# A hybrid decoder layer: convolutions in a lane of their own, longer pauses in the mixer's side work, retention by pairs of heads

## The chip, the cores and the metric

The kernel runs on one core of one Trainium2 chip. The metric is the device time of one execution in microseconds; the kernel before takes 2025.46 us in the median of three runs (2024.82 to 2027.49). Engines are named as in the profile: PE is TensorE (matmul), PEld its weight loads, DVE is VectorE, ACT is ScalarE, POOL is GpSimd, SP is SyncE, which issues most DMAs.

## The reference

One layer for 256 tokens with 2048 features, in float32:

```
x = x + 0.5 * swiglu(rmsnorm(x, n1), ffn1)          # width 5632
x = x + mixer(rmsnorm(x, n2), w_in, w_out)
x = x + 0.5 * swiglu(rmsnorm(x, n3), ffn2)
return rmsnorm(x, n4)

mixer: proj = h @ w_in; rq, rk, rv, rg (retention, 8 heads of 128), gq, gk, gv, gz (delta rule, 8 heads), ga, gb
  rq, rk = rotary(rq), rotary(rk) / sqrt(128)
  ro = layernorm_per_head(sum_{s<=t} gamma_h^(t-s) (q_t . k_s) v_s) * silu(rg)
  gq, gk, gv = silu(causal depthwise convolution over 4 tokens); q, k l2-normalised
  g = -exp(a_log) softplus(ga + dt_bias); beta = sigmoid(gb)
  S_t = exp(g_t) (I - beta_t k_t k_t^T) S_{t-1} + beta_t k_t v_t^T;  go_t = S_t^T q_t
  go = rmsnorm_per_head(go) * gw * silu(gz)
  return concat(ro, go) @ w_out
```

## The kernel before, in words

Every large product streams its weights. A piece of 512 KB (256 rows by 512 columns) is loaded by a DMA of SP into `raw`, ACT rounds it to `whi` (L134), DVE subtracts to get `wlo` (L135), and PE multiplies three times per 128 rows and token half: hi·hi, hi·lo, lo·hi (L148 to L150) into an `acc` bank. One such triple is called a unit here; a piece has four units, and pieces are prepared three ahead of PE. The first FFN comes first, then the mixer, then the second FFN.

The mixer has 16 column blocks of `w_in` of 32 units each, and then the output projection, 4 blocks of 32 units. Everything else in the mixer (convolutions, gates, delta rule, rotation, retention) is side work that rides along: it is written as generators, and after each unit `advance` lets each lane take a step. `yield n` in a generator means: nothing more for n units. Since all engines work in the order of the program, this fixes where each piece of side work stands between the matmuls. `until` advances the lanes without any unit between, when something is needed before the next block.

There are two lanes. `chains` holds, one behind the other, the gates, the three convolutions of head group 1 (K, Q, V; four heads), the delta chain of group 1, then the convolutions and the delta chain of group 2, and the chains that transpose the finished heads for the output projection. `side` holds the rotary tables, the rotation of retention's Q and K, and retention. So the three convolutions of group 2 begin when the delta chain of group 1 has ended, although their blocks may have been there for some time.

`evacuated` runs a block's 32 units and lets ACT write it to SBUF, in a ring of three `pe` buffers. A convolution (`conv_chain`) transposes two heads on PE into an `mx` bank (`mx` has three PSUM banks, `acc` four, `qd` one), ACT multiplies by the last tap (L705), DVE adds three taps per head (L707, runs of three), six units later the next two heads follow, each with its own Silu. The delta chain (`delta_chain`) first makes the decays: sixteen DVE instructions write `gu` (L750), two PE matmuls make `dp` from them (L754). Then come squares and norms, the matrices `Nt` and `At`, a recursion on DVE of two small instructions (`yn`, `Yb`, L837 and L838) per step and one step per unit, and two levels of a block inverse by quads: four `qd` matmuls (L808), one behind each unit (the trace has two records for each), and a DVE instruction that reads the bank: `Pm` (L862), then X or Y. At its end stand the states and the gate (L917). Retention takes its four heads at once.

In the output projection and the second FFN's start, steps of norms and transposes wait in the queue `later`, one of which is issued every second unit.

Of the kernel before, what the change touches and what calls it, by code (L numbers as in the profile page):

```python
# [85 lines left out]
def hybrid_layer(ctx: ExitStack, tc: tile.TileContext, a: dict, out: bass.AP):  # L86
# [10 lines left out]
    mx = ctx.enter_context(tc.tile_pool(name="mx", bufs=3, space=PSUM))  # L97
# [137 lines left out]
    def product(*args):  # L235
        accs, units = product_units(*args)
        for i, _ in enumerate(units):
            if i % 2 and i > 1 and later:
                later.popleft()()
        return accs  # L240
# [161 lines left out]
    def mixer_plan():  # L402
        wi, wo = a["w_in"][0], a["w_out"][0]
        half = RET_W // 2
        for c0 in ([O_GK, O_GQ, O_GV, O_GZ, O_GZ + half, O_RQ] + [o + half for o in (O_GK, O_GQ, O_GV)]
                   + [O_RK, O_RV, O_RG] + [o + half for o in (O_RQ, O_RK, O_RV, O_RG)]):
            whole(wi, rows_of(0, KD), c0)
        pair = [list(product_pieces(OUT_ORDER, wo, b * NB)) for b in range(2)]
        first = 3 * len(pair[0]) // 4
        for part in (slice(0, first), slice(first, None)):  # L410
            for b in range(2):
                stream.add((wo.tensor.name, b * NB), pair[b][part])
        for b in range(2, D // NB):
            whole(wo, OUT_ORDER, b * NB)
# [56 lines left out]
    with tc.manual_schedule(engines={E.PE, E.DVE, E.Activation}), tc.tile_pool(name="gd", bufs=1) as gd:  # L471
        gd.tile([P, PAD], F32, name="pad")

        def mixed_out(o, b, xt=None):
            for t in range(NT):
# [4 lines left out]
        env = dict(x_left=x_left, ident=ident, mx=mx, qd=qd, product=product, product_units=product_units, power=power,  # L480
                   split=split,
                   weight_piece=weight_piece, do_later=do_later, mixed_out=mixed_out,
# [33 lines left out]
def mixer(tc, a, gd, env):  # L516
    nc = tc.nc
    V, S, G, PE = nc.vector, nc.scalar, nc.gpsimd, nc.tensor
    x_left, ident, mx, qd, power = (env[k] for k in ("x_left", "ident", "mx", "qd", "power"))
# [7 lines left out]
    with ExitStack() as ctx:  # L527
# [19 lines left out]
        chains, side = deque(), deque()  # L547
        waits = {id(chains): 0, id(side): 0}

        def advance():  # L550
            for lane in (chains, side):
# [24 lines left out]
        rf, pes, read, PES = [], [], set(), 3  # L576

        def evacuated(col, dst=None, func=AF.Copy):
            ps, units = product_units(x_left, w_in, rows, col)
            run(units)  # L580
            if dst is None:

                until(lambda: len(pes) < PES or id(pes[-PES]) in read)
                dst = pb.tile([P, NT, NB], F32, name="pe", bufs=PES)
                pes.append(dst)
            for t in range(NT):
# [13 lines left out]
        def gates_chain():  # L600
# [21 lines left out]
            yield 7  # L622
# [6 lines left out]
            V.scalar_tensor_tensor(az, z, -1.0, z, ALU.mult, ALU.min)  # L629
            S.activation(az, az, AF.Exp)  # L630
# [4 lines left out]
            S.activation(az, az, AF.Ln, bias=ones)  # L635
            V.scalar_tensor_tensor(z, z, 0.0, az, ALU.max, ALU.add)
            for t in range(NT):
                V.scalar_tensor_tensor(g[:, t, :], z[:, t, :], -1.0, ea, ALU.mult, ALU.mult)
            S.copy(g2[:, 0], g)
            V.tensor_tensor(g2[:, 1], g, g2[:, 0].bitcast(F32), ALU.subtract)  # L640
            V.tensor_scalar(eb, eb, 1.0, None, ALU.add)
            V.reciprocal(beta, eb)

            yield 12
# [10 lines left out]
        def rotary_chain():  # L655
# [17 lines left out]
            for _ in range(2):  # L673
# [4 lines left out]
                for part in parts:  # L678
                    yield 4
                    for tx in (th.bitcast(F32), tl):  # L680
                        V.scalar_tensor_tensor(ang, tx, -part, ang, ALU.mult, ALU.add)
            V.tensor_scalar(ang, ang, -math.pi, math.pi, ALU.max, ALU.min)
            S.activation(sinT, ang, AF.Sin)
            V.scalar_tensor_tensor(ang, ang, -1.0, ang, ALU.mult, ALU.min)
            V.tensor_scalar(ang, ang, math.pi / 2, None, ALU.add)
            S.activation(cosT, ang, AF.Sin)
# [5 lines left out]
        def conv_chain(src, ct0, dst):  # L692
# [3 lines left out]
            dst = dst()  # L696
            for i in range(0, GH, 2):
                pt = mx.tile([P, 2, T], F32, name="mx")
# [3 lines left out]
                for j in range(2):  # L702
                    w = cw[:, ct0 + i + j, :]
                    yy = y[:, i + j, :]
                    S.mul(yy, pt[:, j, :], w[:, 3:4])  # L705
# [31 lines left out]
        gates, mixed = {}, []  # L737

        def delta_chain(gi, ins):

            hs = gi * GH
            kq, vT = ins["kq"], ins["vT"]
# [3 lines left out]
            for h0 in range(0, GH, 2):  # L746
# [4 lines left out]
                yield 2  # L751
# [6 lines left out]
            yield 4  # L758
# [3 lines left out]
            for c in range(NT):  # L762
                if c:
                    yield 2
# [4 lines left out]
            for c in range(NT):  # L769
                yield 2  # L770
                square_sums(tokens(qT, c), ss[:, 1, c * GH:(c + 1) * GH])
            V.tensor_scalar(ss, ss, EPS, None, ALU.add)
# [7 lines left out]
            for c in range(NT):  # L780
                yield 1
# [5 lines left out]
            for j in range(GH):  # L787
                yield 2
# [32 lines left out]
            Yb = gd.tile([P, B0 // RS, B0], F32, name="Yb")  # L821
# [11 lines left out]
            for j in range(B0 - 1):  # L833
# [5 lines left out]
                yield 1  # L839
            yd = dr.tile([NM, P, B0], F32, name="yd")  # L840
# [12 lines left out]
            for lev in range(LEV0, NLEV):  # L853
# [4 lines left out]
                yield 2  # L858
# [4 lines left out]
                if lev < NLEV - 1:  # L863
# [3 lines left out]
                    yield 2  # L867
# [18 lines left out]
            yield 2  # L886
            S.copy(st, four(lambda j: (kd[:, j, :], w[:, 0, j, :])))
            S.copy(o[:, 0], four(lambda j: (At[:, j, 0, :], w[:, 0, j, :])))
            yield 2
# [3 lines left out]
            V.tensor_tensor(o[:, 1], four(lambda j: (qT[:, j, P:], st[:, j, :])), eg1, ALU.mult)  # L893
            yield 3
            V.tensor_tensor(w[:, 1], four(lambda j: (Yv[:, j, 1, :], vh[:, 1, j, :])), bc(ck[:, 1, :]), ALU.mult)
            yield 2
# [22 lines left out]
        def delta_gate(gi):  # L919
            gates[gi] = zs = mk.tile([P, NT, NB], F32, name=f"gate{gi}")  # L920
            evacuated(O_GZ + gi * GW, zs, AF.Silu)
# [4 lines left out]
        def delta_products(gi):  # L926
            hs, cs = gi * GH, gi * GW
            ins = {}

            def kq(part):  # L930
                if part == 0:
                    ins["kq"] = gd.tile([P, GH, 2, T], F32, name="kq")
# [6 lines left out]
            chains.append(conv_chain(evacuated(O_GK + cs), 8 + hs, partial(kq, 0)))  # L939
            chains.append(conv_chain(evacuated(O_GQ + cs), hs, partial(kq, 1)))  # L940
# [180 lines left out]
```

## Time and profile before

| what | us |
|---|---|
| median of three runs | 2025.46 (2024.82 to 2027.49) |
| the profiled execution | 2025.33 |
| its span in the trace | 2023.6 |
| PE busy | 1972.1 |
| PE idle | 51.5 |
| DVE busy | 1289.1 |
| ACT busy | 888.5 |
| POOL busy | 59.7 |

The span is what the trace shows of one execution, the time has 1.7 us more outside it. Busy time is the union of an engine's instructions; the idle time in front of an instruction is put down to what released it. The granted clock of PE (PEclk) is a share of full speed: 1.00 is 2.4 GHz, 0.50 is 1.2 GHz.

### The profile page before, as it was taken

Reading aid. Unit: us, or ns where it says so; the run is one execution under the profiler, and the core shown is the slowest. Engines: PE = TensorE matmul, PEld = TensorE weight load, DVE = VectorE, ACT = ScalarE, POOL = GpSimd, SP = SyncE. Lnnn points to the kernel's source line nnn. Section 1 sums busy time; section 2 is a strip of 40 time slices with the busy share of each in tenths; the row PEclk is TensorE's granted clock in tenths of the full one; section 3 lists DMA queues with packets and bytes.
Section 4 is the critical chain, followed back from the end, with each engine's and each line's share of the span. In section 5 each row is a group of like instructions: output and inputs, shape, how many; then the busy total and the mean of one; then the engine's idle time right before and its main releaser. Section 6 shows DMA issues by size and latency. Waiting matters only on the chain.

```text
span 2023.6 us, 23594 instructions
## 1 busy us (share of the span) xinstructions
PE 1972.1 (97%) x8836; PEld 1620.1 (80%) x8836; DVE 1289.1 (64%) x1818; ACT 888.5 (44%) x1074; POOL 59.7 (3%) x79
## 2 busy tenths in 40 slices
PE   9999999999999999899799999999999999999998
PEld 7888888888888887777677778788888888888886
DVE  5776664456667766675668466866667554667654
ACT  6434433334443555543444344544444434444443
POOL 0000000000000000210021000000000000000000
PEclk9999999999999999999999999999999999999999
DMA  9666666666665655578447735666666666666564
GB/s 310 192 184 187 207 196 195 193 187 185 206 197 184 201 169 182 139 184 154 125 135 163 146 116 178 204 190 197 191 195 187 199 195 191 195 193 192 178 207 145
DMA packets 195267, 373.06 MB, mean 184 GB/s; under 512 B 14544, under 2 KB 15184, under 8 KB 195024
## 3 DMA queue, kind: packets, MB, share of 16 engines
q1 hardware_dynamic: 193888, 368.38, 62.0%
q0 software_dynamic: 832, 1.84, 0.4%
q8 instruction: 69, 1.13, 0.2%
q10 hardware_dynamic: 432, 1.34, 0.2%
q14 instruction: 46, 0.38, 0.1%
HBM read 368.89 MB, written 2.62 MB: 184 GB/s over the span
## 4 chain that ended last, share of the span: by engine, by line
PE 86%; DVE 8%; ACT 3%; issue 2%; DMA 1%; ACTq 0%; POOLq 0%; DVEq 0%
PE acc L148 28%; PE acc L149 27%; PE acc L150 27%; DVE wlo L135 3%; ACT whi L134 2%; DVE y L707 1%; PE qd L808 1%; DMA raw<-in_w_in_dram 1%; DVE y L253 1%; PE mx L731 1%; DVE yn L837 1%; DVE Yb L838 0%; PE mx L791 0%; DVE sq L253 0%; DVE ht L253 0%
## 5 line engine op out<-in xcount | busy, mean ns | idle before, releaser
L135 DVE TENSOR_TENSOR wlo<-raw,whi 128x1024 fp32r<-128x1024 f32 (+1 forms) x689 | 839.5, 1227 | 627.2 <-ACT whi L134 624.9
L134 ACT CAST whi<-raw 128x1024 fp32r<-128x1024 f32 (+1 forms) x689 | 718.4, 1050 | 814.1 <-PE acc L150 720.9
L148 PE MATMUL acc<-whi,xh 128*128 128x512 f32 x1920 | 763.5, 398 | 4.4 <-ACT whi L134 2.4
L149 PE MATMUL acc<-wlo,xh 128*128 128x512 f32 x1920 | 751.9, 392 | 5.0 <-DVE wlo L135 4.9
L150 PE MATMUL acc<-whi,xl 128*128 128x512 f32 x1920 | 750.7, 391 | 0.0
L149 PEld LDWEIGHTS acc<-wlo,xh 128*128 128x128 f32 x1920 | 362.8, 189 | 79.7 <-DVE wlo L135 8.9
L148 PEld LDWEIGHTS acc<-whi,xh 128*128 128x128 f32 x1920 | 362.8, 189 | 78.4 <-ACT whi L134 6.6
L150 PEld LDWEIGHTS acc<-whi,xl 128*128 128x128 f32 x1920 | 362.4, 189 | 76.2
L149 PE MATMUL acc<-wlo,hh 128*128 128x512 f32 x704 | 273.9, 389 | 0.0
L150 PE MATMUL acc<-whi,hl 128*128 128x512 f32 x704 | 273.9, 389 | 0.0
L148 PE MATMUL acc<-whi,hh 128*128 128x512 f32 x704 | 273.9, 389 | 0.0
L253 DVE STREAM_TRANSPOSE ht<-h 32x256 f32<-32x256 f32 x352 | 153.3, 436 | 5.3
L149 PEld LDWEIGHTS acc<-wlo,hh 128*128 128x128 f32 x704 | 132.1, 188 | 27.7 <-DVE wlo L135 0.2
L148 PEld LDWEIGHTS acc<-whi,hh 128*128 128x128 f32 x704 | 132.1, 188 | 27.5
L150 PEld LDWEIGHTS acc<-whi,hl 128*128 128x128 f32 x704 | 132.1, 188 | 27.3
L140 ACT CAST hh<-ht 128x512 fp32r<-128x512 f32 x44 | 27.2, 618 | 121.2 <-DVE ht L253 121.2
L149 PE MATMUL acc<-wlo,mh 128*128 128x512 f32 x96 | 37.7, 393 | 3.1 <-DVE wlo L135 3.0
L141 DVE TENSOR_TENSOR hl<-ht,hh 128x512 fp32r<-128x512 f32 x44 | 30.3, 688 | 15.1 <-ACT hh L140 15.1
L707 DVE SCALAR_TENSOR_TENSOR y<-mx,cw,y 128x255 f32<-128x255 f32 (+2 forms) x72 | 34.6, 481 | 8.2 <-ACT y L705 6.5
L347 ACT ACTIVATE sg<-acc,rfac 128x512 f32<-128x512 f32 x44 | 29.8, 689 | 18.4 <-PE acc L150 16.0
L148 PE MATMUL acc<-whi,mh 128*128 128x512 f32 x96 | 37.4, 390 | 0.0
L150 PE MATMUL acc<-whi,ml 128*128 128x512 f32 x96 | 37.4, 390 | 0.0
(210 smaller groups left out, 759.7 us busy)
## 6 DMA issues: line engine op xcount, KB each, us to landing
raw<-in_ffn_w_up_dram SPq DMA_DIRECT2D x176, 512.0 KB, 4.5
raw<-in_ffn_w_down_dram SPq DMA_DIRECT2D x176, 512.0 KB, 4.5
raw<-in_ffn_w_gate_dram SPq DMA_DIRECT2D x175, 512.0 KB, 4.4
raw<-in_w_in_dram SPq DMA_DIRECT2D x128, 512.0 KB, 4.8
raw<-in_w_out_dram SPq DMA_DIRECT2D x32, 512.0 KB, 3.7
x<-in_x_dram SPq DMA_DIRECT2D x4, 512.0 KB, 6.4
out_dram<-x SPq DMA_DIRECT2D x8, 256.0 KB, 2.4
h<-in_xt_dram SPq DMA_DIRECT2D x7, 256.0 KB, 5.8
```

The source lines that it names most:

```text
L134: S.copy(hi, raw)
L135: V.tensor_tensor(lo, raw, hi.bitcast(F32), ALU.subtract)
L140: S.copy(hi, src)
L141: V.tensor_tensor(lo, src, hi.bitcast(F32), ALU.subtract)
L148: PE.matmul(o, lhsT=sh, rhs=hi, start=first, stop=False)
L149: PE.matmul(o, lhsT=sh, rhs=lo, start=False, stop=False)
L150: PE.matmul(o, lhsT=sl, rhs=hi, start=False, stop=last)
L253: V.transpose(dv[q:q + Q, :, :, r:r + Q], sv[r:r + Q, :, :, q:q + Q])
L347: S.activation(sg[:, t, :], g[t], AF.Silu, scale=rf[:, t:t + 1])
L707: V.scalar_tensor_tensor(yy[:, lag:], pt[:, j, :T - lag], w[:, 3 - lag:4 - lag], yy[:, lag:], ALU.mult, ALU.add)
L731: PE.matmul(pt[:, j, :], lhsT=lhsT, rhs=rhs, start=True, stop=True)
L808: PE.matmul(pt[:m, i, :], lhsT=lhsT, rhs=rhs, start=True, stop=True)
```

## The change

A third lane, `convs`, holds the convolutions alone; they get a PSUM bank of their own, `cv` (one buffer), and `mx` has two banks instead of three. In a convolution ACT's multiplications of both heads come first, the two runs of three stand two and five units behind, the next pair eight units behind the first, and one Silu ends it. The delta chain is queued from the start and waits until its V is there; the second one stands behind the mixed chain of group 1. Most pauses get longer, by one unit or more, and the gates' chain and the rotary tables get pauses where there were none. The block order changes: the second half of GZ moves from ahead of RQ to behind the second group's convolution blocks and RK. The ring of evacuated blocks has two buffers, the two gates share one tile, and `delta_gate`, RV and RG are written to tiles that are asked for only after their units. Retention goes by pairs of heads and writes its result over `v`. The first two blocks of the output projection are walked in four parts by head group, each needing only the heads that it reads, and `later` gives a step every third unit.

```diff
-    mx = ctx.enter_context(tc.tile_pool(name="mx", bufs=3, space=PSUM))
+    mx = ctx.enter_context(tc.tile_pool(name="mx", bufs=2, space=PSUM))
+    cv = ctx.enter_context(tc.tile_pool(name="cv", bufs=1, space=PSUM))
...
+    def beside(units, every=2):
+        for i, _ in enumerate(units):
+            if (i + 1) % every == 0 and i > 1 and later:
+                later.popleft()()
...
-        for c0 in ([O_GK, O_GQ, O_GV, O_GZ, O_GZ + half, O_RQ] + [o + half for o in (O_GK, O_GQ, O_GV)]
-                   + [O_RK, O_RV, O_RG] + [o + half for o in (O_RQ, O_RK, O_RV, O_RG)]):
+        for c0 in ([O_GK, O_GQ, O_GV, O_GZ, O_RQ] + [o + half for o in (O_GK, O_GQ, O_GV)]
+                   + [O_RK, O_GZ + half, O_RV, O_RG] + [o + half for o in (O_RQ, O_RK, O_RV, O_RG)]):
...
-        chains, side = deque(), deque()
+        chains, convs, side = deque(), deque(), deque()
...
-        rf, pes, read, PES = [], [], set(), 3
+        rf, pes, read, PES = [], [], set(), 2
...
             for i in range(0, GH, 2):
-                pt = mx.tile([P, 2, T], F32, name="mx")
+                pt = cv.tile([P, 2, T], F32, name="cv")
                 for j in range(2):
                     for t in range(NT):
                         PE.transpose(pt[:, j, t * P:(t + 1) * P], src[:, t, (i + j) * P:(i + j + 1) * P], ident)
                 for j in range(2):
+                    S.mul(y[:, i + j, :], pt[:, j, :], cw[:, ct0 + i + j, 3:4])
+                if i + 2 == GH:
+                    read.add(id(src))
+                yield 2
+                for j in range(2):
                     w = cw[:, ct0 + i + j, :]
                     yy = y[:, i + j, :]
-                    S.mul(yy, pt[:, j, :], w[:, 3:4])
                     for lag in (1, 2, 3):
                         V.scalar_tensor_tensor(yy[:, lag:], pt[:, j, :T - lag], w[:, 3 - lag:4 - lag], yy[:, lag:],
                                                ALU.mult, ALU.add)
-                if i + 2 == GH:
-                    read.add(id(src))
-                    S.activation(dst, y, AF.Silu)
-                    held.discard("y")
-                yield 6
+                    yield 3
+            S.activation(dst(), y, AF.Silu)
+            held.discard("y")
...
             hs = gi * GH
+            while "vT" not in ins:
+                yield 1
...
-                yield 2
+                yield 4
                 dp = mx.tile([P, 4, P], F32, name="mx")
...
-            chains.append(conv_chain(evacuated(O_GK + cs), 8 + hs, partial(kq, 0)))
-            chains.append(conv_chain(evacuated(O_GQ + cs), hs, partial(kq, 1)))
-            chains.append(conv_chain(evacuated(O_GV + cs), 16 + hs, vT))
-            chains.append(delta_chain(gi, ins))
+            convs.append(conv_chain(evacuated(O_GK + cs), 8 + hs, partial(kq, 0)))
+            convs.append(conv_chain(evacuated(O_GQ + cs), hs, partial(kq, 1)))
+            convs.append(conv_chain(evacuated(O_GV + cs), 16 + hs, vT))
...
-        chains.append(gates_chain())
         side.append(rotary_chain())
-        delta_products(0)
+        chains.append(gates_chain())
+        chains.append(delta_chain(0, ins[0]))
+        delta_products(0, ins[0])
         delta_gate(0)
-        delta_gate(1)
+        chains.append(mixed_chain(NH, gates[0], ["kq"]))
         q0 = rotated(O_RQ, "rqT")
-        delta_products(1)
-        r0 = retention_products(0, q0)
-        chains.append(mixed_chain(NH, gates[0], ["kq"]))
+        delta_products(1, ins[1])
+        chains.append(delta_chain(1, ins[1]))
+        r0 = retention_products(0, q0, lambda: delta_gate(1))
...
-        for _, units in pair:
-            run(islice(units, 3 * GH * NT))
-        until(lambda: not chains and not side)
-        for b, (o, units) in enumerate(pair):
-            deque(units, 0)
-            env["mixed_out"](o, b, pb.tile([P, NB // P, T], F32, name="y" if b else "sq", bufs=1))
+        for i in range(4):
+            until(lambda: len(made) > i)
+            for b, (o, units) in enumerate(pair):
+                part = islice(units, GH * NT)
+                if i < 3:
+                    run(part)
+                    continue
+                env["beside"](part, 3)
+                env["mixed_out"](o, b, pb.tile([P, NB // P, T], F32, name="y" if b else "sq", bufs=1))
```

DVE's order ahead of group 2's `gu`, in the kernel before (L707 is a convolution's tap, L975 the rotation of a `pe` block, L135 the weight stream's subtraction):

```order
L707 SCALAR_TENSOR_TENSOR y<-mx,cw,y 128x255
L707 SCALAR_TENSOR_TENSOR y<-mx,cw,y 128x254
L707 SCALAR_TENSOR_TENSOR y<-mx,cw,y 128x253
L707 SCALAR_TENSOR_TENSOR y<-mx,cw,y 128x255
L707 SCALAR_TENSOR_TENSOR y<-mx,cw,y 128x254
L707 SCALAR_TENSOR_TENSOR y<-mx,cw,y 128x253
L135 TENSOR_TENSOR wlo<-raw,whi 128x1024
L975 TENSOR_TENSOR y<-pe,cosT 128x512 x2
L750 TENSOR_SCALAR gu<-cst,g_5470 128x128 x8
L135 TENSOR_TENSOR wlo<-raw,whi 128x1024
```

The two runs of three of the last pair stand directly ahead of a rotation and `gu`. DVE's order at the same `gu` (now L769) in the changed kernel (L142 splits the transposed heads of group 1 that the mixed chain makes, L787 makes `kd` from the keys):

```order
L938 SCALAR_TENSOR_TENSOR gate<-o,fac,gate 128x128 x8
L136 TENSOR_TENSOR wlo<-raw,whi 128x1024
L142 TENSOR_TENSOR m_7657<-mx,m_7657 128x512
L136 TENSOR_TENSOR wlo<-raw,whi 128x1024
L142 TENSOR_TENSOR m_7657<-mx,m_7657 128x512
L769 TENSOR_SCALAR gu<-cst,g_5473 128x128 x8
L136 TENSOR_TENSOR wlo<-raw,whi 128x1024
L769 TENSOR_SCALAR gu<-cst,g_5473 128x128 x8
L136 TENSOR_TENSOR wlo<-raw,whi 128x1024 x2
L787 TENSOR_TENSOR kd<-mx,eg 128x512
```

No convolution stands near `gu` any more; all of group 2's are far ahead of it. The first of them stands inside group 1's recursion; DVE's order there in the changed kernel, from the last tap of its first run of three to the last of its second (L857 and L858 are the recursion's step, L726 the tap, and behind the second run of three the bank `cv` is free for the next two heads):

```order
L726 SCALAR_TENSOR_TENSOR y<-cv,cw,y 128x253
L857 TENSOR_TENSOR yn<-Ub,Yb 128x75
L858 TENSOR_TENSOR Yb<-Yb,yn 128x5x15
L136 TENSOR_TENSOR wlo<-raw,whi 128x1024
L857 TENSOR_TENSOR yn<-Ub,Yb 128x70
L858 TENSOR_TENSOR Yb<-Yb,yn 128x5x14
L857 TENSOR_TENSOR yn<-Ub,Yb 128x65
L858 TENSOR_TENSOR Yb<-Yb,yn 128x5x13
L726 SCALAR_TENSOR_TENSOR y<-cv,cw,y 128x255
L726 SCALAR_TENSOR_TENSOR y<-cv,cw,y 128x254
L726 SCALAR_TENSOR_TENSOR y<-cv,cw,y 128x253
```

In the kernel before, the recursion has nothing between its steps but the weight stream (four steps, then L135); now the two runs stand between them.

PE's order where group 1's first quad ends and its second begins, in the kernel before (a `whi` with a new number is a new piece, `qd` with a new number is the next quad, which needs the bank that `Pm` has read):

```order
L808 MATMUL qd_7039<-X_7029,Nt_6378 128x64
L148 MATMUL acc_7016<-whi_6974,xh_93 128x512
L149 MATMUL acc_7016<-wlo_6975,xh_93 128x512
L150 MATMUL acc_7016<-whi_6974,xl_94 128x512
L808 MATMUL qd_7039<-X_7029,Nt_6378 128x64
L148 MATMUL acc_7015<-whi_6992,xh_93 128x512
L149 MATMUL acc_7015<-wlo_6993,xh_93 128x512
L150 MATMUL acc_7015<-whi_6992,xl_94 128x512
L808 MATMUL qd_7064<-X_7029,Nt_6378 128x64
```

The two quads meet at the end of a piece. PE's order at the same place in the changed kernel:

```order
L828 MATMUL qd_7196<-X_7177,Nt_6450 128x64
L149 MATMUL acc_7041<-whi_7144,xh_96 128x512
L150 MATMUL acc_7041<-wlo_7145,xh_96 128x512
L151 MATMUL acc_7041<-whi_7144,xl_97 128x512
L828 MATMUL qd_7196<-X_7177,Nt_6450 128x64
L149 MATMUL acc_7042<-whi_7144,xh_96 128x512
L150 MATMUL acc_7042<-wlo_7145,xh_96 128x512
L151 MATMUL acc_7042<-whi_7144,xl_97 128x512
L828 MATMUL qd_7221<-X_7177,Nt_6450 128x64
```

The first quad's last matmul, behind the fourth unit of a piece before, now stands behind the first, and the next quad's first one behind the second.

## Rows read from the trace of the kernel before

**Rows 1.** Page, busy time: us, share of the span, instructions.

```profile
PE 1972.1 (97%) x8836; PEld 1620.1 (80%) x8836; DVE 1289.1 (64%) x1818; ACT 888.5 (44%) x1074; POOL 59.7 (3%) x79
```

**Rows 2.** TensorE by stretch of the mixer: length, busy, granted clock, DMA share, GB/s.

```profile
760.00:780.00 20.00, 17.55 (x72) 0.91 0.47 142
...
980.00:1000.00 20.00, 17.66 (x84) 1.00 0.41 131
1000.00:1020.00 20.00, 7.19 (x21) 0.70 0.36 107
...
1180.00:1220.00 40.00, 36.73 (x188) 1.00 0.41 132
...
1260.00:1298.00 38.00, 33.88 (x146) 1.00 0.55 169
sum 571.00, PE 532.32; mean PE 31.31
```

**Rows 3.** The same table for five short stretches behind idle times.

```profile
774.90:778.30 3.40, 2.64 (x7) 0.63 0.37 81
823.50:829.80 6.30, 6.30 (x22) 0.73 0.74 139
1016.40:1021.40 5.00, 4.63 (x10) 0.50 0.44 149
1109.10:1112.50 3.40, 2.76 (x10) 0.67 0.98 236
1130.50:1133.90 3.40, 3.04 (x9) 0.53 0.88 169
```

**Rows 4.** Waits of TensorE in the mixer: us in total, times, longest.

```profile
PE mx L754 <- DVE gu L750: 16.5, 2, 11.5
PE acc L149 <- DVE wlo L135: 7.3, 7, 1.5
PE mx L987 <- DVE y L980: 4.0, 4, 2.1
PE qd L808 <- DVE Pm L862: 3.1, 2, 2.4
```

**Rows 5.** Timeline around 1016, VectorE, then TensorE: start, us, line, operation.

```profile
1007.61 1.51 DVE L707 SCALAR_TENSOR_TENSOR y<-mx,cw,y 128x255 f32<-128x255 f32 x3 [0.54 <-ACT y L705]
...
1015.76 1.65 DVE L750 TENSOR_SCALAR gu<-cst,g 128x128 fp32r<-128x128 f32 x8
...
1016.77 1.49 PE L754 MATMUL mx<-gu,slr 128*128 128x512 f32 x2 [11.47 <-DVE gu L750]
```

**Rows 6.** Timeline of TensorE at 815: two matmuls of the weight stream.

```profile
815.20 0.39 PE L149 MATMUL acc<-wlo,xh 128*128 128x512 f32 x1
815.42 0.39 PE L150 MATMUL acc<-whi,xl 128*128 128x512 f32 x1
```

**Rows 7.** Timeline of VectorE at 878: one step of the recursion.

```profile
878.06 0.23 DVE L837 TENSOR_TENSOR yn<-Ub,Yb 128x76 f32<-128x76 f32 x1
878.33 0.24 DVE L838 TENSOR_TENSOR Yb<-Yb,yn 128x76 f32<-128x76 f32 x1
```

**Rows 8.** Timeline at 1146: `whi`, `wlo`, `Pm`, the next `qd` matmul.

```profile
1145.19 1.05 ACT L134 CAST whi<-raw 128x1024 fp32r<-128x1024 f32 x1
...
1146.27 1.23 DVE L135 TENSOR_TENSOR wlo<-raw,whi 128x1024 fp32r<-128x1024 f32 x1 [2.47 <-ACT whi L134]
...
1147.41 0.42 DVE L862 TENSOR_TENSOR Pm<-qd,cst 128x256 f32<-128x256 f32 x1
...
1147.89 0.43 PE L808 MATMUL qd<-X,Nt 128*128 128x64 f32 x2 [0.69 <-DVE Pm L862]
```

**Rows 9.** Timeline of VectorE, 1187 to 1195: statistics, gate, scaling.

```profile
1187.07 0.26 DVE L1026 BATCH_NORM_STATS2 bs<-rd 128x6 f32<-128x128 f32 x1
...
1191.17 2.19 DVE L917 SCALAR_TENSOR_TENSOR gate<-o,fac,gate 128x128 f32<-128x128 f32 x8
1193.28 2.14 DVE L1036 TENSOR_SCALAR rd<-rd,mv,rs 128x128 f32<-128x128 f32 x8
```

More of the change, by code (lines that the diff above doesn't have):

```diff
@@ L233, in do_later, with product @@
             later.popleft()()
-    def product(*args):
+    def beside(units, every=2):
+        for i, _ in enumerate(units):
+            if (i + 1) % every == 0 and i > 1 and later:
+                later.popleft()()
+    def product(*args, every=2):
         accs, units = product_units(*args)
-        for i, _ in enumerate(units):
-            if i % 2 and i > 1 and later:
-                later.popleft()()
+        beside(units, every)
         return accs
@@ L404, in mixer_plan @@
         half = RET_W // 2
-        for c0 in ([O_GK, O_GQ, O_GV, O_GZ, O_GZ + half, O_RQ] + [o + half for o in (O_GK, O_GQ, O_GV)]
-                   + [O_RK, O_RV, O_RG] + [o + half for o in (O_RQ, O_RK, O_RV, O_RG)]):
+        for c0 in ([O_GK, O_GQ, O_GV, O_GZ, O_RQ] + [o + half for o in (O_GK, O_GQ, O_GV)]
+                   + [O_RK, O_GZ + half, O_RV, O_RG] + [o + half for o in (O_RQ, O_RK, O_RV, O_RG)]):
             whole(wi, rows_of(0, KD), c0)
         pair = [list(product_pieces(OUT_ORDER, wo, b * NB)) for b in range(2)]
-        first = 3 * len(pair[0]) // 4
-        for part in (slice(0, first), slice(first, None)):
+        n = len(pair[0]) // 4
+        for i in range(0, len(pair[0]), n):
             for b in range(2):
-                stream.add((wo.tensor.name, b * NB), pair[b][part])
+                stream.add((wo.tensor.name, b * NB), pair[b][i:i + n])
         for b in range(2, D // NB):
@@ L574, in hold, with evacuated @@
             held.add(name)
-        rf, pes, read, PES = [], [], set(), 3
-        def evacuated(col, dst=None, func=AF.Copy):
+        rf, pes, read, PES = [], [], set(), 2
+        def evacuated(col, dst=None, func=AF.Copy, free=None):
             ps, units = product_units(x_left, w_in, rows, col)
@@ L585, in evacuated @@
                 pes.append(dst)
+            else:
+                until(free)
+                dst = dst()
             for t in range(NT):
@@ L735, in b4 @@
             return ap.unsqueeze(1).broadcast_to([P, 4, ap.shape[1]])
-        gates, mixed = {}, []
+        gates, mixed, made = {}, [], []
         def delta_chain(gi, ins):
             hs = gi * GH
+            while "vT" not in ins:
+                yield 1
             kq, vT = ins["kq"], ins["vT"]
@@ L919, in delta_gate @@
         def delta_gate(gi):
-            gates[gi] = zs = mk.tile([P, NT, NB], F32, name=f"gate{gi}")
-            evacuated(O_GZ + gi * GW, zs, AF.Silu)
+            gates[gi] = zs = evacuated(O_GZ + gi * GW, partial(mk.tile, [P, NT, NB], F32, name="gate"), AF.Silu,
+                                       lambda: gi == 0 or id(gates[0]) in read)
             for c in range(NT):
@@ L962, in mixed_chain @@
             read.add(id(src))
+            made.append(r0)
         def rotated_chain(src, dst):
@@ L1044, in retention_chain @@
             gate.append(None)
+            done.append(hs)
         def rotated(col, name):
```

123 lines of the change are left out of this document (66 added, 57 removed).

## Prediction

> **What bounds the kernel now.** The page comes first: TensorE (PE) is busy 1972.1 of 2023.6 us [rows 1], so what the change can give is PE's idle time and the time in which PE ran slowly; the number of matmuls is the same in both kernels. The second view is the table of busy time by stretch. The mixer runs from 727 to 1298 us, and in these 571.0 us PE is busy 532.32, so 38.7 us of idle time lie there [rows 2], three quarters of all 51.5. The third view is the granted clock. In five stretches behind long idles PE is granted 0.50 to 0.73 of full speed; one minus the clock, times the length, gives 1.26 + 1.70 + 2.50 + 1.12 + 1.60 = 8.2 us [rows 3]. The mixer so loses about 47 us. More than that the change cannot give, since it touches nothing outside.
>
> The fourth view, PE's waits, says who ends the idle time [rows 4]: VectorE (DVE) every time that matters. DVE is not full (64%), it is handed much at once. The two waits for `gu` are the largest: 16.5 us, of which 11.5 in group 2 and so 5.0 in group 1 [rows 4]. In group 2 the DVE rows show why: the convolution's runs of three (1.51 us) stand in one row ahead of `gu`, with the `wlo` of the weight stream between, and PE's matmul L754 stands still until 1016.77 [rows 5]. Around it, 980 to 1020, PE is idle 2.3 + 12.8 = 15.1 us [rows 2].
>
> **The measure for what follows.** Matmuls of the weight stream start 0.22 to 0.23 us apart at full clock (815.20, 815.42), so a unit of three takes 0.68 us, a weight piece (4 units) 2.72 us [rows 6]. At 0.50 of the clock [rows 3] a matmul costs some 0.2 us more. A piece asks DVE for one `wlo` of 1.23 us, behind which the next instruction starts after 1.14 us [rows 8]; I count 1.13.
>
> **What is removed**, against the 47 us:
> - The row of convolutions, `gu` and L754 in group 2. A lane of their own starts the three convolutions as soon as their blocks are there, and `gu`, which only needs the gates, is issued four units (2.7 us) ahead of L754. 15.1 us idle and 2.5 us of clock go: 17.6.
> - `gu` in group 1: 5.0 idle and 1.7 clock, 6.7.
> - The gates' chain, now in small parts (stretch behind 772): 2.4 idle [rows 2], 1.3 clock, 3.7.
> - The first rotation behind the recursion, 1.6, and the second, 2.4 and 1.1 of clock: 5.1. The waits for `y` in [rows 4] are these.
> - The waits for `Pm` of group 2: 3.1 idle and 1.6 clock, 4.7 [rows 4, 3].
> - `wlo` late behind group 2's recursion: 0.9, one of the seven waits for it that sum to 7.3 [rows 4].
> - The end of the mixed transposes (`m`, `ml`, `pe`): 3.3 [rows 2], which moves and is counted again below.
> - The output projection: 38.0 less 33.88 busy leaves 4.1 [rows 2]; with the deferred steps every third unit (2.04 us) instead of every second (1.36) DVE gets what it needs.
> That is 46. The rest (0.4 at 743, where PE waits for ScalarE) stays.
>
> **What it adds.** None of the new waits stands in the trace of before; each is bounded by rows.
> - *One buffer for the convolutions' transposes (`cv`).* The second pair's transposes are issued 8 units (5.4 us) behind the first's, and the first pair's last run of three is issued at +5 units: 3 units (2.04 us) for 1.51 us of DVE [rows 5]. Alone that holds. A `wlo` of 1.13 between makes it 0.6 late, as soon as one falls there; for three of the six convolutions I take 0.45, and for group 1's second one, where a table load of ScalarE lies ahead, 1.1: 2.5. Bounds: nothing, and 1.13 each, 6.8.
> - *Group 2's first convolution lies over group 1's recursion.* A recursion step is `yn` and `Yb`, 0.27 each, one step a unit [rows 7]. Four steps and a `wlo` are 2.12 + 1.13 = 3.25 us for a piece of 2.72: DVE falls 0.53 us back in each piece, 2.7 us in the five pieces ahead of the convolution. From its first run of three to the end of its second DVE is handed five steps (2.65), one or two `wlo` (1.7) and two runs (2.9): 7.2 us, where PE's next `cv` transposes come 5.4 us behind. PE waits 2.7 + 7.2 − 5.4 = 4.5; I take 4.1, since not every instruction of these stretches follows without a pause on the one before. Behind a wait of 5.0 the clock cost 1.7 [rows 3]; I take 2. Sum 6.1; bounds 0 and 6.5.
> - *The quads of the triangular inverse (`qd`, one PSUM buffer).* In group 1 a quad's last matmul now stands behind the first unit of a piece and no longer behind the last, as the order of PE shows. At that place DVE has just begun the piece's `wlo` (ScalarE's `whi` starts with the piece and takes 1.05 [rows 8]), so `Pm` starts 2.25 us into the piece and ends at 2.67, while PE wants the buffer 1.84 us in. The nearest row is 1146 to 1148: there `wlo` came late, `Pm` stood behind it, and PE's next `qd` matmul waited 0.69, about 0.95 against its due place [rows 8]. Here it is 0.85 to 1.45 with a run of three between; six quads at 1.15 give 7. Bounds: 0 (if `Pm` comes first) and 9.
> - *The gate of group 2 and the transposes behind it.* In the 16 units (10.9 us) ahead, DVE is handed the statistics (eight of 0.26 with a short fold behind each, 3.2), the scaling L1056 (2.14 as L1036 in before), the gate's run of eight (2.19) [rows 9], the last product (two, 1.3) and four `wlo` (4.5) and some small ones: 14.5. Of the 3.6 excess I take 2.5 as idle, with 1.0 of clock: 3.5; 0.75 more for `mx` having two buffers. Bounds 0 and 6. Without any of it the removed 3.3 above is all gain.
> - The rest, all with DVE a little late: `dp` 0.7, `wlo` beside it 0.4, the rotations 0.7, the 0.4 that stays: 2.2.
> The sum is 2.5 + 6.1 + 7 + 4.25 + 2.2 = 22. The mixer's loss falls from 47 to 22, so 25 us are won: 2025.3 − 25 = **2000** us. The profiled execution is 0.1 us from the median of the runs shown, so no correction is made.
>
> *Costed at nothing:* the new order of the blocks with two buffers for evacuated blocks (a block's last reader is through before the second next one is evacuated, 64 units later), retention by pairs of heads (the same products, `o` written over `v`), the output projection's first pair in quarters (each quarter's operand is issued before the units that read it), and the weight stream on SP, whose pieces keep their number and lead: between 36 and 55% of the DMA time is used in the stretches shown [rows 2]. If a cover is gone, steps are issued with no units between them, as at 1005, at the price of that wait.
>
> **The rivals.**
> - *The new waits don't show.* DVE has 36% free, and PE takes the weights three pieces ahead. If the convolution, the quads and the gate cost nothing, 5 of the 22 are left: 1983. For it: in before the recursion put DVE some 4 us back (7.5 pieces by 0.53), which cost PE only 0.9. Against: here PE waits for the buffer itself.
> - *The clock.* Six idles of over 1 us in some 30 units, with the `cv` wait not far ahead, could take PE to 1.2 GHz for that stretch: 30 × 3 matmuls × 0.2 = 18 us more, 2018. Against it: PE's waits for `wlo` were up to 1.5 us long, two of these in the output projection, and the granted clock from 1260 to 1298 stayed 1.00 [rows 4, 2]; the half clock came behind idles of 2.1, 2.4, 5.0 and 11.5 us and behind 772's two that add up to 2.4. The Trainium skill ("TensorE: Matmul & The Clock Gate", section "A second HAM failure mode: psum-queue depth-cycling") tells of a kernel in which short idles between groups of matmuls, from cycling through PSUM buffers, made the clock go up and down and lowered the throughput; that speaks against fewer `mx` buffers and a single `cv`. By that rule the time is this rival's; the rows so far don't bear it out.
> - *The second `dp` still waits for `gu`*, so that the change does only half of what it says: as in group 1 of before, 5.0 + 1.7 = 6.7 more, 2007.
> - *Slower: the single `cv` buffer.* If each of the six convolutions pays the 6.1 that I give only to one, the sum grows by 5 × 6.1 − 2.5 = 28: 2028. It decides from 25/5 + 0.5 = 5.5 us for each of the other five. Against it: only one lies over a recursion.
>
> **How the numbers follow.** A measurement of this kernel tells about 0.2%, 4 us, from no change. Forecast (1994 to 2006) 0.47; new waits hidden (1981 to 1994) 0.20; `dp` again 0.08; the clock (2010 to 2019) 0.15; no change 0.05; slower 0.05. Forecast, hidden waits, `dp` and clock all end below 2021: faster 0.90. The range for 8 in 10 leaves out the best of the hidden case and the worst of the clock's with what lies above: 1984 to 2015; it holds the lower and most of the upper bounds above (0 and +6.5, 9, 6 against 6.1, 7, 4.25).
>
> **What would show it.** In the trace after: no wait for `gu` above 1 us, PE idle in the mixer near 18 and half clock for about 4; a wait of 3 to 5 us for `cv` at the first convolution of group 2, and some six waits near 1 us at L828 in group 1. The prediction is wrong where waits for `cv` come at every convolution, where the granted clock falls in group 1's quads, or where PE waits for `wlo` for microseconds, since then DVE is fuller than these rows say.

## The result and the profile after

The changed kernel takes 2003.74 us in the median of four runs (2002.66 to 2004.88), the kernel before 2026.47 in its four (2024.82 to 2027.74): a ratio of 0.9888, 95% interval 0.9871 to 0.9905, so 22.7 us faster. The forecast was 2000 with 1984 to 2015. The profiled execution took 2002.66 us, its span is 2000.8. One of the ten executions of the kernel with the lane undone, below, took 2828 us at a granted clock of 0.65, and its ratio leaves that one out.

The page's first lines of the changed kernel, as in [rows 1]:

```profile
span 2000.8 us, 23620 instructions
...
PE 1966.6 (98%) x8836; PEld 1618.0 (81%) x8836; DVE 1289.9 (64%) x1818; ACT 892.4 (45%) x1075; POOL 61.8 (3%) x79
```

PE's idle time is 2000.8 − 1966.6 = 34.2 us, where it was 51.5. The stretch that answers to 727 to 1298 now ends at 1276. The table by stretch of the changed kernel (length, busy, granted clock, DMA share, GB/s), to be read beside [rows 2, 3]:

```profile
885.00:900.00 15.00, 11.69 (x48) 0.89 0.75 136
...
930.00:968.00 38.00, 32.76 (x166) 1.00 0.52 124
...
1000.00:1020.00 20.00, 18.09 (x80) 0.91 0.48 139
...
1085.00:1100.00 15.00, 11.69 (x50) 0.99 0.75 170
1100.00:1115.00 15.00, 15.00 (x63) 0.90 1.01 181
...
1180.00:1200.00 20.00, 18.23 (x88) 1.00 0.45 155
...
1240.00:1276.20 36.20, 36.20 (x162) 1.00 0.64 208
sum 549.20, PE 527.18; mean PE 27.75
```

In 549.2 us PE is busy 527.18: 22.0 us idle, where it was 38.7. The clock costs 0.11 × 15 + 0.09 × 20 + 0.01 × 15 + 0.10 × 15 = 5.1, where it was 8.2. The loss fell from 47 to 27 us. These 20 us explain most of the 22.7. About 1 us lies outside the mixer (1452.6 us there before, 1451.6 now), and the other 2 are busy time of PE in the mixer that went beyond what the clock accounts for; what they are is not shown. The output projection (1240 to 1276) has no idle time left.

PE's waits in the mixer of the changed kernel, to be read beside [rows 4]:

```profile
PE qd L828 <- DVE Pm L883: 4.5, 5, 1.2
PE cv L716 <- DVE yn L857: 3.3, 1, 3.3
PE mx L1007 <- DVE y L1000: 2.4, 2, 2.0
PE mx L773 <- DVE gu L769: 2.1, 3, 1.7
PE mx L979 <- DVE gate L938: 1.8, 2, 1.0
PE cv L716 <- ACT whi L135: 1.6, 3, 0.5
PE qd L828 <- DVE X L872: 1.2, 1, 1.2
PE cv L716 <- DVE y L726: 1.1, 1, 1.1
...
PE acc L150 <- DVE wlo L136: 0.9, 2, 0.5
...
PE mx L622 <- issue: 0.5, 1, 0.5
```

`gu` fell from 16.5 us to 2.1 and `wlo` from 7.3 to 0.9; the new waits, at `cv` and at `qd`, stand where they were forecast. The releasers are inferred: the three waits at `cv` put down to `whi` go when the convolutions get more banks (cv_shared, below), those put down to `pe` do not. The longest wait, first on VectorE with the two runs of three ahead of it, then on PE:

```profile
886.02 1.51 DVE L726 SCALAR_TENSOR_TENSOR y<-cv,cw,y 128x255 f32<-128x255 f32 x3
...
889.93 1.51 DVE L726 SCALAR_TENSOR_TENSOR y<-cv,cw,y 128x255 f32<-128x255 f32 x3
```

```profile
891.58 0.66 PE L716 MATMUL cv<-ident,pe 128*128 128x128 f32 x2 [3.31 <-DVE yn L857]
```

The second run ends at 891.4, 5.4 us behind the start of the first, and PE's transposes start with it.

### The profile page after: what moved, and what is told of

Same layout as the page of the kernel before. It is cut to its first block, busy times and chain, and to the rows that moved or that the text cites. A ratio compares the mean times of both kernels' runs of the same rounds, so it can differ in the third digit from the quotient of the medians.

```text
span 2000.8 us, 23620 instructions
## 1 busy us (share of the span) xinstructions
PE 1966.6 (98%) x8836; PEld 1618.0 (81%) x8836; DVE 1289.9 (64%) x1818; ACT 892.4 (45%) x1075; POOL 61.8 (3%) x79
## 4 chain that ended last, share of the span: by engine, by line
PE 48%; DVE 4%; issue 1%; ACT 1%; DMA 0%; POOLq 0%; DVEq 0%; ACTq 0%
PE acc L149 15%; PE acc L151 15%; PE acc L150 15%; DVE wlo L136 1%; ACT whi L135 1%; PE mx L748 1%; PE qd L828 0%; DVE yn L857 0%; DVE Yb L858 0%; DMA raw<-in_ffn_w_down_dram 0%; DVE rv L1056 0%; PE mx L1025 0%; DVE gu L769 0%; PE mx L979 0%; PE mx L811 0%
## 5 line engine op out<-in xcount | busy, mean ns | idle before, releaser
L135 ACT CAST whi<-raw 128x1024 fp32r<-128x1024 f32 (+1 forms) x689 | 720.3, 1051 | 818.3 <-PE acc L151 741.7
L142 DVE TENSOR_TENSOR hl<-ht,hh 128x512 fp32r<-128x512 f32 x44 | 30.3, 688 | 15.1 <-ACT hh L141 15.1
L726 DVE SCALAR_TENSOR_TENSOR y<-cv,cw,y 128x255 f32<-128x255 f32 (+2 forms) x72 | 34.6, 480 | 3.0 <-ACT y L718 1.2
```

What stands on the lines that cost most here:

```text
L135: S.copy(hi, raw)
L142: V.tensor_tensor(lo, src, hi.bitcast(F32), ALU.subtract)
L726: V.scalar_tensor_tensor(yy[:, lag:], pt[:, j, :T - lag], w[:, 3 - lag:4 - lag], yy[:, lag:], ALU.mult, ALU.add)
```

## The experiments

Each kernel is compared with the kernel before on its own chip; the kernel before ran between 2026.5 and 2028.1 in the median there. A difference between two kernels from different chips therefore carries up to 1.6 us of the chips.

**The phase of group 1's quads.** Four kernels differ in one number. All start group 2's delta chain four units later (`gu4`); the other three also move group 1's quads by one, two and three units, and make it up behind them, so that nothing else moves. The diff is that of phase3, with one of its two shortened pauses; in phase2 the 4 is 3 and one pause is shortened, in phase0 it is 5 and three are; gu4 has the first two edits alone.

```diff
             while "vT" not in ins:
                 yield 1
+            if gi:
+                yield 4
...
-            yield 28
+            yield 24 if gi else 28
...
-            yield 2
+            yield 2 if gi else 4
             X = gd.tile([P, NM, P], F32, name="X")
...
-            yield 3
+            yield 3 if gi else 2
             S.copy(st, four(lambda j: (kd[:, j, :], w[:, 0, j, :])))
```

Expected of gu4, phase2, phase3 and phase0:

> The changed kernel, but group 2's delta chain starts four units later (and makes them up in a pause of 28 units, now 24), so that its gu stands 2.7 us later. In the changed kernel eight gu took 3.82 us beside a GpSimd product of 2.53 us on the gate, where the same eight took 1.65 us in the kernel before, and TensorE waited 1.7 + 0.2 us for them. Theory: GpSimd's product slows VectorE; out of its way, gu takes 1.65 again, the wait falls to 0.4 or less, and with the clock that it cost the time falls by 2 to 3 us, to about 2001. Rival: gu is late for the work queued ahead of it (gate, two splits); then it stays at some 2 us of wait and 2003 to 2004.

> As gu4, and group 1's quads stand one unit later (made up in a pause behind them), so that a quad ends behind the second unit of a piece. In the changed kernel the six waits at the qd matmuls of group 1 add up to 5.2 us. Theory: they come from wlo standing ahead of Pm on VectorE; here Pm is 0.2 us late, the six add up to 0 to 1.5, and the time is 4 us below gu4. Rival: one qd bank costs a round trip wherever the quad stands; then they stay at about 5 us and the time is that of gu4.

> As gu4, and group 1's quads stand two units later: a quad ends behind the third unit of a piece, when wlo is through. Theory (wlo ahead of Pm): the six waits add up to under 0.5 us, and the time is 5 us below gu4, near 1996. Rival (one bank's round trip): about 5 us of waits, the time of gu4.

> As gu4, and group 1's quads stand three units later: a quad ends behind the last unit of a piece, as it did in the kernel before. Theory (wlo ahead of Pm): under 0.5 us of waits, 5 us below gu4, near 1996, unless the convolution's runs of three fall into the gap. Rival (one bank's round trip): about 5 us of waits, the time of gu4.

Measured: gu4 2004.52 us (ratio to before 0.9888, 0.9873 to 0.9902), phase2 1998.88 (0.9857, 0.9843 to 0.9872), phase3 1997.15 (0.9851, 0.9834 to 0.9867), phase0 1996.54 (0.9852, 0.9834 to 0.9870). PE's waits from 925 to 972, first gu4:

```profile
PE qd L830 <- DVE Pm L885: 3.9, 4, 1.2
PE qd L830 <- DVE X L889: 0.9, 1, 0.9
PE qd L830 <- DVE Y L899: 0.4, 1, 0.4
```

phase2, phase3 and phase0, in this order:

```profile
PE qd L830 <- DVE Pm L885: 0.5, 2, 0.3
```

```profile
PE mx L748 <- DVE w L908: 0.6, 1, 0.6
PE qd L830 <- DVE X L889: 0.4, 1, 0.4
PE qd L830 <- DVE Pm L885: 0.2, 1, 0.2
```

```profile
PE mx L748 <- DVE w L908: 1.2, 1, 1.2
```

The waits at `qd` are 5.2, 0.5, 0.6 and 0 us. The times follow by 5.6 to 8 us; phase2 is the cleanest pair, since PE's first gates' matmul (L622) waits 2.1 us in it as in gu4, while it waits 1.6 us less in phase3's profile and 0.7 less in phase0's. One bank and its round trip are the same in all four; what differs is where the read of the bank stands beside the `wlo` in VectorE's queue. In the changed kernel (gu4 has the same):

```profile
931.93 1.23 DVE L136 TENSOR_TENSOR wlo<-raw,whi 128x1024 fp32r<-128x1024 f32 x1 [2.01 <-ACT whi L135]
...
933.08 0.42 DVE L883 TENSOR_TENSOR Pm<-qd,cst 128x256 f32<-128x256 f32 x1
...
933.55 0.43 PE L828 MATMUL qd<-X,Nt 128*128 128x64 f32 x2 [0.94 <-DVE Pm L883]
```

`Pm` begins when `wlo` is through, and PE waits for it. In phase2 `Pm` still follows a `wlo`, but PE comes a unit later and waits 0.3 us at most; in phase3 three of the four `Pm` begin only after VectorE itself has waited 0.5 to 1.1 us for PE. The rival falls. What comes back is 0.6 and 1.2 at L748, where the pauses were shortened to make up the units.

For `gu`, VectorE's eight `gu` and GpSimd's product on the gate in the changed kernel:

```profile
1002.89 3.82 DVE L769 TENSOR_SCALAR gu<-cst,g 128x128 fp32r<-128x128 f32 x8
```

```profile
1002.92 2.53 POOL L945 TENSOR_TENSOR gate<-gate,gnw 128x512 f32<-128x512 f32 x2 [6.61 <-ACT gate L597]
```

and the same two in gu4, two lines of its stretches, and a wait:

```profile
1009.04 1.64 DVE L771 TENSOR_SCALAR gu<-cst,g 128x128 fp32r<-128x128 f32 x8
```

```profile
1005.47 2.57 POOL L947 TENSOR_TENSOR gate<-gate,gnw 128x512 f32<-128x512 f32 x2 [6.58 <-ACT gate L597]
```

```profile
1000.00:1020.00 20.00, 19.17 (x89) 1.00 0.48 145
...
1180.00:1200.00 20.00, 18.22 (x79) 0.91 0.41 134
```

```profile
PE mx L622 <- issue: 2.1, 1, 2.1
```

Beside GpSimd eight `gu` take 3.82 us, alone 1.64: 2.18 us longer for 2.53 us of GpSimd. In gu4 a `wlo` lies beside the product instead and takes 2.17 us for 1.23, but PE does not wait for it there. The waits for `gu` fell from 2.1 to 1.0 us (the longest from 1.7 to 0.4) and the granted clock of the stretch rose from 0.91 to 1.00, some 2.9 us together, as the theory said. Yet the time didn't fall: in gu4's profile L622 waited 2.1 us, where it was 0.5 in the changed kernel's, and behind the last gate the clock stood at 0.91 where the changed kernel's had 1.00, for the same two waits of 1.0 and 0.8 us. Neither place was changed, and L622 waits between 0.4 and 2.1 us in the profiles of these kernels; so of gu4 the mechanism is shown and the gain in time is not.

**One part alone: a deferred step every third unit**, in the kernel before.

```diff
-    def product(*args):
+    def product(*args, every=2):
         accs, units = product_units(*args)
         for i, _ in enumerate(units):
-            if i % 2 and i > 1 and later:
+            if (i + 1) % every == 0 and i > 1 and later:
                 later.popleft()()
...
-            o = product(m_left, a["w_out"][0], OUT_ORDER, b * NB)
+            o = product(m_left, a["w_out"][0], OUT_ORDER, b * NB, every=3)
```

> The kernel before, with one part of the change alone: in the output projection's last two blocks a deferred step every third unit instead of every second. In the kernel before TensorE is idle 4.1 us from 1260 to 1298, waiting for wlo and x. Theory: DVE is handed too much there; at every third unit these waits go, and the time falls by 3.5 to 4.5 us, to about 2022.5. Rival: the steps that no longer fit run together at the start of the second FFN, where TensorE waits for them instead; then the time stays at 2026.

Measured 2021.88 us beside 2027.61 (0.9972, 0.9962 to 0.9983): 5.7 us faster, by its interval 3.4 to 7.7. From 1250 to 1290 PE has no idle time:

```profile
1250.00:1290.00 40.00, 40.00 (x178) 1.00 0.62 192
```

Nor has it any from 1290 to 1310 (20.0 busy of 20), so the deferred steps do not pile up there; this part of the sum (4.1) agrees.

**The lane undone**, in the changed kernel.

```diff
-        chains, convs, side = deque(), deque(), deque()
+        chains, side = deque(), deque()
...
-            convs.append(conv_chain(evacuated(O_GK + cs), 8 + hs, partial(kq, 0)))
+            chains.append(conv_chain(evacuated(O_GK + cs), 8 + hs, partial(kq, 0)))
...
-        chains.append(delta_chain(0, ins[0]))
         delta_products(0, ins[0])
+        chains.append(delta_chain(0, ins[0]))
```

> The changed kernel with the convolutions put back into the lane of the delta chains, in the order of the kernel before; all else stays, the ring of two evacuated blocks too. Group 2's convolutions then wait for group 1's delta chain, and the block that needs a free buffer of the ring lets the rest of that chain run without units between: three quads, the states, the gate and two transposes. Theory: some 20 round trips of TensorE and VectorE of 1 to 1.5 us each stand bare, 20 to 30 us, and the time is 2024 to 2036, so that the lane carries the whole gain. Rival: the longer pauses and the parts of the output projection carry most of it, and the time stays below 2012.

Measured 2028.91 us beside 2027.61 (1.0007, 0.9997 to 1.0016): the whole gain is gone. Its largest waits, and the stretch in which the rest of group 1's delta chain is run off bare, with no units between:

```profile
PE cv L716 <- DVE y L726: 12.5, 6, 4.0
PE mx L979 <- DVE gate L938: 7.3, 2, 6.7
```

```profile
920.00:1010.00 90.00, 64.11 (x294) 0.79 0.33 82
```

PE is busy 64.1 of 90 us, and the clock is 0.79. The size came as expected, the reason only in part: of the 25.9 us of idle time, eleven waits of the bare chain are 12.7, the wait for X ahead of it is 2.6, and five waits at `cv` are 10.6 (970 to 1006), where group 2's convolutions run close behind one another through their single bank. That the lane alone brings 23 us does not follow: the kernel before has a ring of three and three `mx` banks, and the lane was not tried alone in it. The run shows that the ring of two, the single bank and the new order need the lane.

**One bank or three**, and **the convolution behind the recursion**. The first puts the convolutions' transposes into `mx` with three banks, in the changed kernel; the second lets group 2's first convolution wait for the recursion, on top of phase3.

```diff
-    mx = ctx.enter_context(tc.tile_pool(name="mx", bufs=2, space=PSUM))
-    cv = ctx.enter_context(tc.tile_pool(name="cv", bufs=1, space=PSUM))
+    mx = ctx.enter_context(tc.tile_pool(name="mx", bufs=3, space=PSUM))
+    cv = mx
...
-                pt = cv.tile([P, 2, T], F32, name="cv")
+                pt = cv.tile([P, 2, T], F32, name="mx")
```

```diff
+            while not ready():
+                yield 1
             yield from hold("y")
...
+            ins["solved"] = True
             yield 1
             yd = dr.tile([NM, P, B0], F32, name="yd")
```

> The changed kernel with the convolutions' transposes back in the mx pool, which has three banks again (no cv bank). In the changed kernel TensorE's waits at cv add up to 6.9 us, 3.3 of them in group 2's first convolution over the recursion. Theory: the single bank makes TensorE wait for VectorE; with three banks 1.5 us or less of these waits are left, and with the clock behind the long one the time falls by 5 to 7 us, to about 1998. Rival: VectorE is late by itself over the recursion; then TensorE waits as long a little later, for wlo or for the next bank, and the time stays at 2003.

> As phase3, and group 2's first convolution waits until group 1's recursion is through (18 units later). Theory: the 3.3 us wait at cv comes from recursion and convolution lying over each other on VectorE; apart, it goes, with the half clock behind it (1.6 us): about 4.5 us below phase3, near 1992.5. Rival: the backlog of the recursion itself delays the first run just as much; then 2 to 3 us of wait stay at cv and the time is within 2 us of phase3.

Measured: cv_shared 1998.86 us (0.9859, 0.9844 to 0.9874), conv_late 1993.72 (0.9838, 0.9821 to 0.9854), 3.4 below phase3 and, by the two ratios, 2.6. In cv_shared all waits of convolutions for VectorE and for `whi` are gone, and one for X has come:

```profile
PE qd L828 <- DVE X L872: 3.3, 2, 2.1
...
PE mx L716 <- ACT pe L597: 1.0, 2, 0.7
```

X had one wait of 1.2 in the changed kernel; the added 2.1 is at group 1's first quad. So 5.9 us of waits go, 2.1 come back and the half clock behind the long wait goes (0.11 × 15 above): 5.4 us, beside 4.9 between the medians. The 1.0 us for `pe` stays with three banks, so it is no cost of the single bank. In conv_late the long wait is gone too, but the later convolutions now stand closer together:

```profile
PE cv L718 <- DVE y L728: 3.8, 4, 1.2
```

So 3.3 us and one wait of 0.5 went, and 2.7 more of this kind came (3.8 where it was 1.1). With the half clock behind the long wait (0.11 × 15 in phase3, none in conv_late) that makes some 2.8 us. The gain lies between what theory (4.5) and rival (under 2) had said; the intervals of conv_late and phase3 overlap, so the waits decide here, not the time.

**What adds up.** `both` is phase3 with three banks; `both_late` has the late convolution besides; `both_rot` is `both` with ten units for six between the rotation's VectorE work and its transposes; `all` has the late convolution, the ten units and two units more ahead of the last gate's transposes.

```diff
-            yield 6
+            yield 10
             rv = r.rearrange("p t h a d -> p t h (a d)")
...
-                yield 4
+                yield 6 if i == 0 and r0 == NH + GH else 4
                 pt = mx.tile([P, 2, T], F32, name="mx")
```

> Phase3 and cv_shared together: group 1's quads two units later, group 2's gu four later, and one pool of three mx banks for the convolutions too. Theory: the waits at cv (6.9 us in the changed kernel) and at group 1's quads (5.2 us) are separate, so the gains add up: some 5 us below phase3, near 1991.5. Rival: without the stop at cv, VectorE's backlog goes on into the quads, where cv_shared showed a wait of 2.1 us for X; then the time stays above 1994.

> As both, with group 2's first convolution behind the recursion, as in conv_late. Theory: the two edits cure the same wait, so the second gives nothing more: within 1.5 us of both. Rival: VectorE's backlog itself costs time elsewhere; then 2 us or more below both.

> As both, with four units more (10 for 6) between the rotation's last VectorE work and TensorE's transposes of it. Theory: the waits for y at unit 1487 (2.0 and 0.3 us) and the half clock behind them (1.5 us) go: 3 to 4 us below both, near 1988. Rival: what comes behind, the scores of retention, now meets its own data late, and the time is that of both.

> As both_rot, with the late convolution, and two units more between the last gate and its transposes (waits of 1.0 and 0.8 us). Theory: these waits go too; 1 to 2 us below both_rot, near 1986. Rival: the following quarter of the output projection then waits for its rows, and the time is that of both_rot.

Measured: both 1989.74 us (0.9814, 0.9799 to 0.9829), both_late 1986.69 (0.9803, 0.9786 to 0.9819), both_rot 1989.14 (0.9811, 0.9797 to 0.9826), all 1985.88 (0.9794, 0.9779 to 0.9808). The gains of phase and banks add up (7.4 below phase3). The late convolution is 3 us faster by the medians, with overlapping intervals. The profiles speak for the theory (nothing more): PE's waits in the mixer sum to 11.9 us in both and 11.4 in both_late, and behind the same wait of 2 us for `y` the clock fell in one and not in the other (0.96 and 1.00 from 1085 to 1120), which neither edit reaches. The time alone decides nothing. The rotation's pause gives nothing, and the waits say where it went. `both` first, then `both_rot`:

```profile
PE mx L1009 <- DVE y L1002: 2.4, 2, 2.1
PE qd L830 <- DVE X L874: 2.1, 2, 1.2
```

```profile
PE qd L830 <- DVE X L874: 4.8, 2, 3.6
```

The 2.4 us for `y` went, and X's wait rose by 2.7. ScalarE shows why, in `both_rot`:

```profile
1092.03 1.05 ACT L135 CAST whi<-raw 128x1024 fp32r<-128x1024 f32 x1 [1.17 <-DMA raw<-in_w_in_dram]
1095.61 1.05 ACT L135 CAST whi<-raw 128x1024 fp32r<-128x1024 f32 x1 [2.53 <-DMA raw<-in_w_in_dram]
...
1105.21 1.04 ACT L135 CAST whi<-raw 128x1024 fp32r<-128x1024 f32 x1 [2.11 <-DMA raw<-in_w_in_dram]
```

and in `both` at the same place:

```profile
1095.59 1.05 ACT L135 CAST whi<-raw 128x1024 fp32r<-128x1024 f32 x1 [1.67 <-PE acc L151]
```

In `both` ScalarE's `whi` waits for PE (a buffer); in `both_rot`, where PE did not stop, it waits up to 2.5 us for the weights themselves. X stands behind a late `wlo` on VectorE, and so it began only 0.5 us earlier (1103.61 for 1104.13), though PE came to it 3 us earlier. From 1085 to 1106 the DMA is full (last but one column), in `both` and in `both_rot`:

```profile
1085.00:1106.00 21.00, 19.82 (x86) 0.94 1.01 179
```

```profile
1085.00:1106.00 21.00, 17.37 (x81) 0.99 1.02 188
```

There the wait for `y` cost nothing, since the weights would not have come sooner. By queue it is the weights themselves that fill the DMA: in `both` the packets of SP's queue take 98.4% of its time in this stretch, those of GpSimd's queue, which carries the recursion's round trip through DRAM, 2.8%. A piece of weights lands 8.3 us after its issue there, and 4.8 in the median of all pieces of `w_in`. Why the weights take longer there was not tested; the round trip's last transfer is under way at the same time.

`all` is the fastest: 2.1% below the kernel before and 17.9 us below the changed one. It is 3.3 us below both_rot by two edits that were not parted: the waits for the gate fell from 1.8 to 0.6 us as expected, with no new wait in the output projection, and that for X from 4.8 to 3.7.

## Why the prediction was right, point by point

- *The loss of before* (47 us) and *what is removed* (46) were read rightly: in the output projection no wait is left, `m`, `ml` and `pe` of the mixed transposes are gone, `wlo` nearly so. One sign did not come: a wait for `gu` of 1.7 us stands where none above 1 was to be, and idle time and half clock are 22.0 and 5.1 for the 18 and 4 named. For the output projection 4.1 was counted, and alone it measured 5.7 with 4.1 inside its interval.
- *The convolution over the recursion*: 4.1 idle and 2 of clock forecast, 3.3 and 1.65 measured. The forecast said that DVE is behind by the recursion and two runs; the trace shows just this chain (886 to 891.4), and with the convolution behind the recursion the wait is gone.
- *The quads*: 1.15 for each, 7 in all; measured 0.4 to 1.2, together 5.2, without any loss of clock (1.00 from 930 to 968). The place of the `wlo` as the cause is shown by the phases.
- *The single bank* elsewhere: 2.5 forecast, three of 0.52 and one of 1.05 measured, 2.6. The long one is at group 1's first convolution, where the rotary tables' steps stand between on VectorE (759.7 to 763.7), and not at the second behind a table load: the size was right, the place and its reason were not.
- *The gate*: 4.25 forecast, 1.8 measured; the clock did not fall in this profile, in gu4's it did.
- *Mis-sized, "the rest, all with DVE a little late"* (2.2 us). `dp` was 0.7 and measured 2.1 idle + 1.8 of clock: `gu` ran beside GpSimd's product on the gate, which the sum did not look at. The rotations were 0.7 and measured 2.4 + 1.6, again behind VectorE work beside GpSimd (four instructions between 1084.16 and 1087.9 took 1.9 us more than their like); this is read from the trace and was not tested. Group 2's quads were counted at nothing and measured 1.8 (1.2 of them for X), the convolutions' wait for `pe` likewise, 1.0; `wlo` and L622 add 0.5 each. That is some 10 us too little, against 5.4 too much at quads, gate and convolution. The loss of 27 for 22 is 5 us off, and the time only 3.7, since some 3 us went that the tables do not count. That the number came so close is in part luck of opposite errors; the mechanisms of the large terms are not.
- *The weight stream, costed at nothing*, held here: none of PE's waits in the mixer is put down to a DMA. But the reason given, a DMA used to 36 to 55%, takes the calm stretches: the forecast's own [rows 3] have 0.98 and 0.88, and from 900 to 940 us the share before was 1.02. `both_rot` shows what lies there.
- *The rivals.* That the new waits don't show is out: at `cv` (without `pe`) and `qd` alone they are 13 us. The clock rival is out: six idles of 0.4 to 1.2 us in 38 us left it at 1.00. By the Trainium skill's section on the cycling of PSUM buffers ("TensorE: Matmul & The Clock Gate", "A second HAM failure mode: psum-queue depth-cycling"), which tells of a kernel in which frequent short idles did this, it would have gone up and down there; this trace does not show it for these idles. That `dp` still waits came true in part (2.1 us, where group 1's wait before was 5.0), by another cause. The single bank did not cost 6 us for each of the other five convolutions but 1.05 once, 0.5 three times and nothing once.

## What to carry to other kernels

When side work is placed by hand between matmuls, look at the place in the helper engine's queue, not only at its load: an instruction that PE waits for must not stand behind the weight stream's own, and one unit of shift was worth 5 us. Where two consumers of VectorE lie over each other, price both remedies, more banks and a later start: here the banks were worth about 5 us and the later start about 3, the banks and the quads' phase added up, and the later start on top of the banks showed no clear gain. And before a wait is removed, look at what it hides: at 1085 to 1106 the weights' DMA was full, and a wait of 2.4 us came back as one of 2.7.

## What the runs showed of the hardware that was not expected

- VectorE beside GpSimd: eight `gu` 3.82 us for 1.64; a recursion step's product 0.64 us for 0.22 (1084.16, beside the rotation's products on GpSimd). The Trainium skill says ("SBUF — State Buffer", section "🔬 SBUF: two separate sides") that the two share a port that one of them locks for a whole instruction. The traces agree in kind: 2.18 us longer for 2.53 us of GpSimd. What the engines share is not seen in them.

```profile
1083.65 0.22 DVE L857 TENSOR_TENSOR yn<-Ub,Yb 128x60 f32<-128x60 f32 x1
...
1084.16 0.64 DVE L857 TENSOR_TENSOR yn<-Ub,Yb 128x54 f32<-128x54 f32 x1
```

- The granted clock behind the same two idles of 1.0 and 0.8 us (at the last gate's transposes, 1180 to 1200) was 1.00 in the changed kernel's profile and 0.91 over the same 20 us in gu4's.
